# Inner columns of eight experts in chunks of 2048 and 1536 instead of 1024, 1024, 1024 and 512

## The chip, the cores and the metric

The kernel runs on one NeuronCore of a Trainium2 chip. The metric is the time of one execution on the device in microseconds (us). TensorE (PE in the profile) multiplies, PEld is its loading of the stationary operand, VectorE is DVE, ScalarE is ACT, GpSimd is POOL and SyncE is SP, which in this kernel issues nearly all DMAs. Results of TensorE land in PSUM, of which there are eight banks of 2 KB per partition; everything else lives in SBUF, 128 partitions wide.

## The reference, cut to what matters

One sequence of 256 tokens, 1024 wide, goes through two layers, all in float32. Layer 0 is attention with a sliding window and a dense SwiGLU block. Layer 1 is sparse attention and then a mixture of eight SwiGLU experts, of which each token uses two:

```
D_MODEL, SEQ, D_FF, N_EXPERTS, TOP_K = 1024, 256, 3584, 8, 2
...
# per expert e, for the tokens t that chose it, with weight g[t, e]:
y[t] += g[t, e] * (silu(x[t] @ w_gate[e]) * (x[t] @ w_up[e])) @ w_down[e]
x = layer_norm(alpha * x + y)
```

Each expert has three matrices of 1024 x 3584 numbers, 14 MB each (1 MB here is 1,048,576 bytes). All eight together are 336 MB, all of which are read once.

## The kernel before

About the first 510 us are attention, the dense block and the choice of experts. The rest is `run_experts`, which handles the eight experts one after the other (e0 to e7 in the order in which they run), and a short end with the LayerNorm.

**Tokens.** The tokens of an expert are gathered into a transposed tile Th by a product with a 0/1 matrix (`gather`). An expert has room for 96 or for 64 tokens: in order of running 96, 64, 96, 96, 64, 96, 96, 64. The first 64 are multiplied as "halves", two column ranges of the weights side by side on TensorE, and the last 32, where there are any, as "quarters", four ranges side by side. The helper `two` runs both steps over the same weights and swaps their order from call to call. The quarters of e0 stand behind a condition that was not met in the profiled run.

**Chunks.** The 3584 inner columns are cut by WIDE into chunks. For a chunk the gate product runs over all 1024 rows, then what is late (`finish`: the combination of the expert before, and `turn`, which transposes h, the hidden values, of the chunk before), then ACT applies Silu to the gate product, TensorE runs the up product, DVE multiplies the two into h, and then comes the down product of the chunk before (`back`). So the down product is always one chunk late.

**Loads.** The weights come as parts of up to 2048 columns in each of 128 partitions, 1 MB, into a rotation of buffers in three pools, raw, more and later. SP's queue issues them in `load` (L173), in the order in which they are needed: gate, up, and down of the chunk before. `take` hands out parts and lets `load` issue the next, up to `ahead` parts in advance, 15 in this stage. A gate or up part of a chunk of 1024 columns has two rows of 4096 bytes per partition, in the chunk of 512 columns four rows of 2048 bytes; a down part has 8192 bytes in a row:

```
order.append((lambda r=r: src()[r:r + n * P, cols], n, width, False, 1, near))
...
src = src().rearrange("(p k) f -> p k f" if near else "(k p) f -> p k f", p=P)
```

Here `near` is true for down alone. A product takes all the parts of its chunk at once, at most four. The names of lines: L1227 is the halves and L1235 the quarters of gate and up, L1252 and L1258 those of down, L1294 the transposes in `turn`, L1295 ACT's copy of them into hTa, L1278 and L1281 Silu, L1286 DVE's product, L1289 its transpose of the quarters' hidden values, L1168 and L1169 the combination, L352 and L353 the LayerNorm at the end.

**Order.** TensorE's order is the order of the program in this stage; those of the other engines are set by the scheduler.

Of the kernel before, what the change touches and what calls it, by code (L numbers as in the profile page):

```python
# [15 lines left out]
OP = mybir.AluOpType  # L16
# [31 lines left out]
WIDE = (1024, 1024, 1024, 512)  # L48
# [36 lines left out]
def trunk(ctx: ExitStack, tc: tile.TileContext, a, out, dbg=None):  # L85
# [57 lines left out]
    def room():  # L143

        state["ahead"] = RAW + sum(kind[3] for kind in extra) - max(WIDE) * KT // PART

# [937 lines left out]
    class Expert:  # L1084
# [63 lines left out]
        def combine(self, ya, yb):  # L1148

            cap = self.cap  # L1150
            y = moe.tile([CAP, D], F32, name="y", bufs=1)[:cap]
# [25 lines left out]
    def run_experts(jobs):  # L1177
# [38 lines left out]

        def gate_up(pa, pb, x, wide):
            T = x.T
            if pb is not None:
                cleared(pb[:, :wide // 4], x)  # L1220
            parts = [w for (w,) in take(KT * wide // PART, 0)]
            n = PART // wide

            def halves():
                for k in range(KT):
                    for h in range(2):
                        PE.matmul(pa[h * CA:(h + 1) * CA, :wide // 2], T[:, k, :CA],  # L1227
                                  parts[k // n][:, k % n, h * wide // 2:(h + 1) * wide // 2],
                                  start=k == 0, stop=k == KT - 1)

            def quarters():
                for k in range(KT):
                    w = parts[k // n][:, k % n].rearrange("p (b q f) -> p q b f", q=4, f=2 * CB)
                    for q in range(4):
                        PE.matmul(pb[q * CB:(q + 1) * CB, :wide // 4].rearrange("p (b f) -> p b f", f=2 * CB),  # L1235
                                  T[:, k, CA:], w[:, q], start=k == 0, stop=k == KT - 1)

            two(x, halves, quarters if pb is not None else None)

        def down(c, hT, ya, yb, x, between=None):  # L1240
# [3 lines left out]
            parts = [w for (w,) in take(n // 2, 0)]  # L1244
# [4 lines left out]
            def halves():  # L1249
                for f in range(n):  # L1250
                    for o in range(2):
                        PE.matmul(ya[o * CA:(o + 1) * CA, :], hT[0][:, f % (n // 2), f // (n // 2), :],  # L1252
                                  parts[f // 2][:, f % 2, o * 512:(o + 1) * 512], **ends(f))

            def quarters():
                for f in range(n):
                    for q in range(4):
# [172 lines left out]
    def job(e):  # L1430
        def follow(c):
            if c == 1 and e + 1 < len(experts):
                experts[e + 1].pick()
# [67 lines left out]
```

## Time and profile before

| what | value |
|---|---|
| median of 3 runs | 1374.52 us (1373.12 to 1375.53) |
| the profiled execution | 1376.65 us, span of its trace 1374.8 us |
| granted TensorE clock, mean | 0.984 of full speed |
| TensorE busy | 1319.6 us, 96% |
| DVE, ACT busy | 441.5 us, 342.8 us |
| bytes moved by DMA | 434.86 MB (of a million bytes) in 129791 packets |

All times come from the profiled execution unless the median is named. Its trace starts with the first instruction, so a place in the program is given as us from the start. The expert stage lies between 514.8 and 1355.7 us, and about 19 us follow it. A busy TensorE is one that has a matmul under way, whichever clock it was granted.

### The profile page before, as it was taken

The page shows a single profiled execution, that of the slowest core. Times are in us where ns is not written, and L with a number is a line of the kernel's source. Part 1 is how long each engine was busy: PE and PEld are TensorE (multiplying, and loading weights), DVE is VectorE, ACT ScalarE, POOL GpSimd, SP SyncE. Part 2 cuts the span into 40 slices and gives each one's busy share as a digit, 9 for nine tenths or more (in the row PEclk, how much of TensorE's full clock was granted, in tenths as well). Part 3 has the DMA queues.
Part 4 walks back from the last instruction along what each step waited for, and adds up shares of the span by engine and source line. Part 5 has one row for each costly group of instructions (what it writes and reads, how often), then busy time and mean ns, then how long its engine had stood idle before and what let it go on. Part 6 is the DMA issues. An engine that isn't in the chain of part 4 may idle for free. (4 is left out here: it accounts for less than half of the span.)

```text
span 1374.8 us, 21889 instructions
## 1 busy us (share of the span) xinstructions
PE 1319.6 (96%) x9035; PEld 756.0 (55%) x9036; DVE 441.5 (32%) x1015; ACT 342.8 (25%) x783; POOL 8.2 (1%) x16
## 2 busy tenths in 40 slices
PE   9999999999999999988889999999999999999994
PEld 6777888888787883432324354454343454435331
DVE  6776555555979853011002001100100100200203
ACT  5755444443558821100001001000101000100100
POOL 0000000000000000000000000000000000000000
PEclk9999999999999999999999999999999999999997
DMA  9515565555364169999999999999999999999994
GB/s 357 186 63 207 175 189 186 186 181 185 124 238 150 63 260 360 408 409 412 407 412 411 405 412 412 408 401 392 414 404 411 413 405 410 411 407 383 412 407 177
DMA packets 129791, 434.86 MB, mean 316 GB/s; under 512 B 11376, under 2 KB 18192, under 8 KB 115728
## 3 DMA queue, kind: packets, MB, share of 16 engines
q1 hardware_dynamic: 123952, 427.81, 80.3%
q10 hardware_dynamic: 5728, 5.50, 1.2%
q8 instruction: 79, 1.29, 0.4%
q14 instruction: 32, 0.26, 0.1%
HBM read 432.23 MB, written 1.05 MB: 315 GB/s over the span
## 5 line engine op out<-in xcount | busy, mean ns | idle before, releaser
L123 DVE TENSOR_TENSOR lo<-raw,hi 128x512 fp32r<-128x512 f32 (+2 forms) x244 | 166.3, 730 | 110.6 <-ACT hi L122 110.6
L1227 PE MATMUL ps<-more,Th 128*64 128x512 f32 (+1 forms) x920 | 188.3, 557 | 4.1 <-DMA more<-in_moe_w_up 2.3
L122 ACT ACTIVATE hi<-raw 128x512 fp32r<-128x512 f32 (+2 forms) x244 | 145.7, 659 | 147.8 <-PE ps L211 133.1
L209 PE MATMUL ps<-hi,Th 128*128 128x512 f32 (+1 forms) x432 | 171.1, 396 | 1.4 <-ACT Th L122 1.4
L211 PE MATMUL ps<-hi,Tl 128*128 128x512 f32 (+1 forms) x432 | 167.3, 388 | 1.4 <-DVE Tl L123 1.4
L210 PE MATMUL ps<-lo,Th 128*128 128x512 f32 (+1 forms) x432 | 167.7, 388 | 0.0
L1286 DVE TENSOR_TENSOR h<-h,ps 128x512 f32<-128x512 f32 (+1 forms) x32 | 19.8, 620 | 357.7 <-PE ps L1227 357.7
L1227 PE MATMUL ps<-later,Th 128*64 128x512 f32 (+1 forms) x680 | 129.4, 526 | 3.3 <-DMA later<-in_moe_w_up 2.1
L1227 PEld LDWEIGHTS ps<-more,Th 128*64 128x64 f32 x920 | 65.3, 138 | 114.9 <-issue 96.3
L1278 ACT ACTIVATE h<-ps 128x512 f32<-128x512 f32 (+1 forms) x32 | 17.4, 543 | 383.8 <-PE ps L1227 367.0
L1252 PE MATMUL ps<-more,hTa 128*64 128x512 f32 x408 | 92.0, 594 | 3.2 <-DMA more<-in_moe_w_down 2.9
L1227 PE MATMUL ps<-raw,Th 128*64 128x512 f32 (+1 forms) x448 | 91.5, 551 | 3.0 <-DMA raw<-in_moe_w_gate 2.5
L209 PEld LDWEIGHTS ps<-hi,Th 128*128 128x128 f32 x432 | 81.6, 189 | 20.5 <-ACT Th L122 2.6
L211 PEld LDWEIGHTS ps<-hi,Tl 128*128 128x128 f32 x432 | 81.5, 189 | 19.9 <-DVE Tl L123 2.5
L210 PEld LDWEIGHTS ps<-lo,Th 128*128 128x128 f32 x432 | 81.6, 189 | 16.3 <-issue 0.2
L1227 PEld LDWEIGHTS ps<-later,Th 128*64 128x64 f32 x680 | 47.5, 137 | 75.4 <-issue 60.3
L1285 DVE TENSOR_TENSOR hb<-hb,ps 128x256 f32<-128x256 f32 (+1 forms) x20 | 7.8, 388 | 212.3 <-PE ps L1235 168.5
L1252 PE MATMUL ps<-later,hTa 128*64 128x512 f32 x312 | 71.0, 596 | 4.3 <-DMA later<-in_moe_w_down 4.0
L1252 PEld LDWEIGHTS ps<-more,hTa 128*64 128x64 f32 x408 | 29.0, 137 | 61.6 <-issue 56.4
L1227 PEld LDWEIGHTS ps<-raw,Th 128*64 128x64 f32 x448 | 31.4, 137 | 55.6 <-issue 44.3
L1235 PE MATMUL ps<-more,Th 128*32 128x256 f32 (+1 forms) x928 | 50.3, 364 | 4.2 <-DMA more<-in_moe_w_gate 4.2
L1252 PEld LDWEIGHTS ps<-later,hTa 128*64 128x64 f32 x312 | 22.1, 137 | 49.2 <-issue 40.8
(260 smaller groups left out, 1370.0 us busy)
## 6 DMA issues: line engine op xcount, KB each, us to landing
more<-in_moe_w_up SPq DMA_DIRECT2D x53, 1024.0 KB, 18.1
more<-in_moe_w_down SPq DMA_DIRECT2D x51, 1024.0 KB, 17.2
more<-in_moe_w_gate SPq DMA_DIRECT2D x50, 1024.0 KB, 19.0
later<-in_moe_w_down SPq DMA_DIRECT2D x38, 1024.0 KB, 16.9
later<-in_moe_w_gate SPq DMA_DIRECT2D x36, 1024.0 KB, 18.2
later<-in_moe_w_up SPq DMA_DIRECT2D x35, 1024.0 KB, 18.4
raw<-in_moe_w_gate SPq DMA_DIRECT2D x26, 1024.0 KB, 20.0
raw<-in_moe_w_up SPq DMA_DIRECT2D x24, 1024.0 KB, 18.6
```

What stands on the lines that cost most here:

```text
L122: state["act"] = ACT.activation(hi, src, AF.Copy)
L123: DVE.tensor_tensor(lo, src, hi.bitcast(F32), op=OP.subtract)
L209: PE.matmul(ps, xh, wh, start=first, stop=False)
L210: PE.matmul(ps, xh, wl, start=False, stop=False)
L211: PE.matmul(ps, xl, wh, start=False, stop=last)
L1227: PE.matmul(pa[h * CA:(h + 1) * CA, :wide // 2], T[:, k, :CA], parts[k // n][:, k % n, h * wide // 2:(h + 1) * wide // 2], start=k == 0, s ...
L1235: PE.matmul(pb[q * CB:(q + 1) * CB, :wide // 4].rearrange("p (b f) -> p b f", f=2 * CB), T[:, k, CA:], w[:, q], start=k == 0, stop=k == KT ...
L1252: PE.matmul(ya[o * CA:(o + 1) * CA, :], hT[0][:, f % (n // 2), f // (n // 2), :], parts[f // 2][:, f % 2, o * 512:(o + 1) * 512], **ends(f))
L1278: ACT.activation(plain(ha, P), paired(ga[:, :wide // 2], P), AF.Silu)
L1285: DVE.tensor_tensor(plain(hb, CB), plain(hb, CB), paired(ub[:, :wide // 4], CB), op=OP.mult)
L1286: DVE.tensor_tensor(plain(ha, P), plain(ha, P), paired(ua[:, :wide // 2], P), op=OP.mult)
```

## The change

WIDE becomes (2048, 1536). A gate or up part is now one row of 8192 or 6144 bytes per partition, so that a part holds 128 rows of a chunk, 1 MB or 768 KB. An expert has 8 + 8 + 6 + 6 gate and up parts and 14 of down, 46 in all, where it had 42. A new constant ATONCE = 4 is the number of parts that a product takes at once: a gate or up product is made in two calls of `two` over four parts each, and a down product in two calls over four (three) parts each. `ahead` stays at 15.

Gate and up of a chunk now need two PSUM banks for the halves and one for the quarters each, where they had one and one; h, hTa and hTb are twice as wide and have one buffer instead of two. `turn` makes 8 or 6 transposes in two banks. The next expert's gather, which stood between the third chunk's down and the last chunk, now stands right before that expert's first gate product. The load of the LayerNorm's gain and bias stays at the end of the last chunk of the last expert. The tiles that sort the tokens share a buffer with y, to make room.

```diff
-WIDE = (1024, 1024, 1024, 512)
+WIDE = (2048, 1536)
+ATONCE = 4
...
-        state["ahead"] = RAW + sum(kind[3] for kind in extra) - max(WIDE) * KT // PART
+        state["ahead"] = RAW + sum(kind[3] for kind in extra) - ATONCE
...
+        def spans(n):
+            return slice(0, 512), slice(512, n)
         def gate_up(pa, pb, x, wide):
             T = x.T
             if pb is not None:
                 cleared(pb[:, :wide // 4], x)
-            parts = [w for (w,) in take(KT * wide // PART, 0)]
-            n = PART // wide
-            def halves():
-                for k in range(KT):
-                    for h in range(2):
-                        PE.matmul(pa[h * CA:(h + 1) * CA, :wide // 2], T[:, k, :CA],
-                                  parts[k // n][:, k % n, h * wide // 2:(h + 1) * wide // 2],
-                                  start=k == 0, stop=k == KT - 1)
-            def quarters():
-                for k in range(KT):
-                    w = parts[k // n][:, k % n].rearrange("p (b q f) -> p q b f", q=4, f=2 * CB)
-                    for q in range(4):
-                        PE.matmul(pb[q * CB:(q + 1) * CB, :wide // 4].rearrange("p (b f) -> p b f", f=2 * CB),
-                                  T[:, k, CA:], w[:, q], start=k == 0, stop=k == KT - 1)
-            two(x, halves, quarters if pb is not None else None)
+            for k0 in range(0, KT, ATONCE):
+                parts = [w[:, 0, :] for (w,) in take(ATONCE, 0)]
+                def halves():
+                    for k, w in enumerate(parts, k0):
+                        for ps, s in zip(pa, spans(wide // 2)):
+                            for h in range(2):
+                                PE.matmul(ps[h * CA:(h + 1) * CA, :s.stop - s.start], T[:, k, :CA],
+                                          w[:, h * wide // 2 + s.start:h * wide // 2 + s.stop],
+                                          start=k == 0, stop=k == KT - 1)
+                def quarters():
+                    for k, w in enumerate(parts, k0):
+                        w = w.rearrange("p (b q f) -> p q b f", q=4, f=2 * CB)
+                        for q in range(4):
+                            PE.matmul(pb[q * CB:(q + 1) * CB, :wide // 4].rearrange("p (b f) -> p b f", f=2 * CB),
+                                      T[:, k, CA:], w[:, q], start=k == 0, stop=k == KT - 1)
+                two(x, halves, quarters if pb is not None else None)
         def down(c, hT, ya, yb, x, between=None):
             if yb is not None and c == 0:
                 cleared(yb[:, :256], x)
             n = WIDE[c] // P
-            parts = [w for (w,) in take(n // 2, 0)]
             def ends(f):
                 return dict(start=c == 0 and f == 0, stop=c == len(WIDE) - 1 and f == n - 1)
-            def halves():
-                for f in range(n):
-                    for o in range(2):
-                        PE.matmul(ya[o * CA:(o + 1) * CA, :], hT[0][:, f % (n // 2), f // (n // 2), :],
-                                  parts[f // 2][:, f % 2, o * 512:(o + 1) * 512], **ends(f))
-            def quarters():
-                for f in range(n):
-                    for q in range(4):
-                        PE.matmul(yb[q * CB:(q + 1) * CB, :256], hT[1][:, f, :],
-                                  parts[f // 2][:, f % 2, q * 256:(q + 1) * 256], **ends(f))
-            two(x, halves, quarters if yb is not None else None, between)
+            for f0 in (0, n // 2):
+                parts = [w for (w,) in take(n // 4, 0)]
+                def halves():
+                    for i in range(n // 2):
+                        f = f0 + i
+                        for o in range(2):
+                            PE.matmul(ya[o * CA:(o + 1) * CA, :], hT[0][:, f % (n // 2), f // (n // 2), :],
+                                      parts[i // 2][:, i % 2, o * 512:(o + 1) * 512], **ends(f))
+                def quarters():
+                    for i in range(n // 2):
+                        f = f0 + i
+                        for q in range(4):
+                            PE.matmul(yb[q * CB:(q + 1) * CB, :256], hT[1][:, f, :],
+                                      parts[i // 2][:, i % 2, q * 256:(q + 1) * 256], **ends(f))
+                two(x, halves, quarters if yb is not None else None, between if f0 else None)
...
-                ga, gb = bank(), bank() if rest else None
+                ga, gb = [bank() for _ in range(2)], bank() if rest else None
                 gate_up(ga, gb, x, wide)
                 finish()
-                ha = later.tile([P, 512], F32, name="h", bufs=2)[:, :wide // 2]
-                hT = [later.tile([P, 4, 2, CA], F32, name="hTa", bufs=2)[:, :wide // 256]]
-                ACT.activation(plain(ha, P), paired(ga[:, :wide // 2], P), AF.Silu)
+                ha = later.tile([P, 1024], F32, name="h", bufs=1)[:, :wide // 2]
+                hT = [later.tile([P, 8, 2, CA], F32, name="hTa", bufs=1)[:, :wide // 256]]
+                for ps, s in zip(ga, spans(wide // 2)):
+                    ACT.activation(plain(ha[:, s], P), paired(ps[:, :s.stop - s.start], P), AF.Silu)
                 if rest:
-                    hb = later.tile([P, 256], F32, name="hb", bufs=1)[:, :wide // 4]
+                    hb = later.tile([P, 512], F32, name="hb", bufs=1)[:, :wide // 4]
                     ACT.activation(plain(hb, CB), paired(gb[:, :wide // 4], CB), AF.Silu)
-                ua, ub = bank(), bank() if rest else None
+                ua, ub = [bank() for _ in range(2)], bank() if rest else None
                 gate_up(ua, ub, x, wide)
                 if rest:
                     DVE.tensor_tensor(plain(hb, CB), plain(hb, CB), paired(ub[:, :wide // 4], CB), op=OP.mult)
-                DVE.tensor_tensor(plain(ha, P), plain(ha, P), paired(ua[:, :wide // 2], P), op=OP.mult)
+                for ps, s in zip(ua, spans(wide // 2)):
+                    DVE.tensor_tensor(plain(ha[:, s], P), plain(ha[:, s], P), paired(ps[:, :s.stop - s.start], P),
+                                      op=OP.mult)
                 if rest:
-                    hT.append(later.tile([P, 8, CB], F32, name="hTb", bufs=2)[:, :wide // P])
+                    hT.append(later.tile([P, 16, CB], F32, name="hTb", bufs=1)[:, :wide // P])
                     DVE.transpose(hT[1].rearrange("p b s -> p (b s)"), hb)
                 def turn(ha=ha, hT=hT, n=wide // 256):
-                    ps = bank().rearrange("p (j q) -> p j q", j=4)
-                    for j in range(n):
-                        PE.transpose(ps[:, j, :], ha[:, j * P:(j + 1) * P], ident)
-                    ACT.activation(hT[0], ps[:, :n].rearrange("p j (h s) -> p j h s", h=2), AF.Copy)
+                    for j0 in range(0, n, 4):
+                        m = min(4, n - j0)
+                        ps = bank().rearrange("p (j q) -> p j q", j=4)[:, :m]
+                        for j in range(m):
+                            PE.transpose(ps[:, j, :], ha[:, (j0 + j) * P:(j0 + j + 1) * P], ident)
+                        ACT.activation(hT[0][:, j0:j0 + m], ps.rearrange("p j (h s) -> p j h s", h=2), AF.Copy)
...
+    sorting = moe.tile([P, D], F32, name="sorting", tag="y", bufs=1)
+    is_at, tmp = (sorting[:, k * NE * NE:(k + 1) * NE * NE].rearrange("p (a b) -> p a b", a=NE) for k in range(2))
+    key, rank = (sorting[:, k * 128:k * 128 + NE] for k in (1, 2))
...
+            if c == 0 and e + 1 < len(experts):
+                experts[e + 1].pick()
             if c == 1 and e + 1 < len(experts):
-                experts[e + 1].pick()
-            if c == 2 and e + 1 < len(experts):
                 experts[e + 1].gather()
-            if c == 3 and e + 1 == len(experts):
+            if c == 1 and e + 1 == len(experts):
                 del extra[:]
                 load_more()
-            if e == 0 and c == 2:
+            if e == 0 and c == 0:
```

With the new chunks, the loads on SP's queue stand in another order. These are SP's rows before the change, from e0's first parts to e1's first gate part (rows without a number are in order; rows that load or compare registers are left out as "..."):

```order
L173 DMA raw<-in_moe_w_gate 128x2x1024 x4
L173 DMA raw<-in_moe_w_up 128x2x1024 x3
L173 DMA more<-in_moe_w_up 128x2x1024
...
L173 DMA later<-in_moe_w_gate 128x4x512 x2
...
L173 DMA raw<-in_moe_w_up 128x4x512 x2
...
L173 DMA raw<-in_moe_w_down 128x2048
L173 DMA more<-in_moe_w_down 128x2048
...
L173 DMA more<-in_moe_w_down 128x2048 x2
...
L173 DMA more<-in_moe_w_gate 128x2x1024
```

And after, the same place:

```order
L174 DMA raw<-in_moe_w_gate 128x2048 x7
...
L174 DMA more<-in_moe_w_up 128x2048 x5
...
L174 DMA later<-in_moe_w_gate 128x1536 x3
...
L174 DMA later<-in_moe_w_up 128x1536 x3
...
L174 DMA later<-in_moe_w_down 128x2048 x2
...
L174 DMA raw<-in_moe_w_down 128x2048 x3
L174 DMA more<-in_moe_w_down 128x2048
...
L174 DMA more<-in_moe_w_down 128x2048 x2
L174 ISA
L174 DMA more<-in_moe_w_gate 128x2048
```

Before, the last chunk's parts and four of down stand ahead of the next expert's gate, and two of down remain; now eight of down stand there, and six remain.

TensorE's rows at the start of e5, the sixth expert to run, a 96-token one behind a 64-token one. Before (the last two rows of e4's down and e5's gate and up product; the second number of a shape is the columns of one matmul):

```order
L1252 MATMUL ps<-more,hTa 64x512 x16
L1235 MATMUL ps<-more,Th 32x256 x8
L1235 MATMUL ps<-later,Th 32x256 x24
L1227 MATMUL ps<-more,Th 64x512 x4
L1227 MATMUL ps<-later,Th 64x512 x12
L1294 MATMUL ps<-cf,h 128x128 x2
L1227 MATMUL ps<-later,Th 64x512 x8
L1227 MATMUL ps<-raw,Th 64x512 x8
L1235 MATMUL ps<-later,Th 32x256 x16
L1235 MATMUL ps<-raw,Th 32x256 x16
```

After, from the end of the gather that now stands in front:

```order
L1145 MATMUL ps<-shares,pickb 96x3
L1241 MATMUL ps<-later,Th 32x512 x16
L1233 MATMUL ps<-later,Th 64x512 x20
L1233 MATMUL ps<-raw,Th 64x512 x12
L1241 MATMUL ps<-later,Th 32x512 x4
L1241 MATMUL ps<-raw,Th 32x512 x12
L1309 MATMUL ps<-cf,h 128x128 x6
L1241 MATMUL ps<-more,Th 32x512 x16
L1233 MATMUL ps<-more,Th 64x512 x28
```

The quarters (L1241) and the halves (L1233) of a gate product now alternate over its two groups of four parts, and six transposes of e4's last chunk (L1309) stand where two did.

ACT's rows in a 96-token expert, where a chunk follows another. Before:

```order
L1281 ACTIVATE hb<-ps 128x256
L1278 ACTIVATE h<-ps 128x512
L1295 ACTIVATE hTa<-ps 128x512
L1278 ACTIVATE h<-ps 128x512
L1281 ACTIVATE hb<-ps 128x256
```

After, from the end of a gather on, with the Silu of the quarters into hb and of the halves into h:

```order
L1142 ACTIVATE back<-ps 96x256
L1292 ACTIVATE hb<-ps 128x512
L1310 ACTIVATE hTa<-ps 128x512
L1310 ACTIVATE hTa<-ps 128x256
L1289 ACTIVATE h<-ps 128x512 x2
```

The copies into hTa now come before the Silu of the halves, and there are two of each.

## Rows read from the trace of the kernel before

**Rows 1.** The page's first part: the span, and TensorE's busy time.

```profile
span 1374.8 us, 21889 instructions
...
PE 1319.6 (96%) x9035; PEld 756.0 (55%) x9036; DVE 441.5 (32%) x1015; ACT 342.8 (25%) x783; POOL 8.2 (1%) x16
```

**Rows 2.** Stretches: busy us of each engine, granted clock, DMA share, GB/s.

```profile
527.00:698.00 171.00, 152.22 (x778) 59.60 (x774) 16.70 (x44) 13.16 (x28) 0.00 (x0) 1.00 1.02 409
527.00:1353.00 826.00, 796.57 (x6252) 341.31 (x6248) 77.32 (x167) 65.99 (x132) 0.00 (x0) 0.99 1.02 407
702.00:711.00 9.00, 6.87 (x46) 2.25 (x44) 0.00 (x0) 0.38 (x1) 0.00 (x0) 0.62 1.03 410
716.00:1024.00 308.00, 308.00 (x2654) 138.06 (x2654) 31.12 (x66) 26.46 (x52) 0.00 (x0) 1.00 1.02 407
1043.00:1336.00 293.00, 293.00 (x2550) 129.14 (x2548) 29.09 (x56) 24.08 (x47) 0.00 (x0) 1.00 1.02 406
```

**Rows 3.** TensorE's waits, 690 to 1375 us: total us, times, longest.

```profile
PE ps L1235 <- DMA more<-in_moe_w_gate: 4.2, 4, 1.5
PE ps L1235 <- DMA later<-in_moe_w_gate: 3.9, 3, 1.5
...
PE ps L1252 <- DMA later<-in_moe_w_down: 1.8, 3, 0.7
```

**Rows 4.** Stretches with one packet size, as in rows 2.

```profile
634.00:641.00 7.00, 5.44 (x26) 1.54 (x24) 0.69 (x1) 0.00 (x0) 0.00 (x0) 1.00 1.01 421
721.00:738.00 17.00, 17.00 (x174) 6.93 (x172) 2.96 (x5) 2.79 (x5) 0.00 (x0) 1.00 1.02 408
672.00:681.00 9.00, 7.88 (x54) 5.03 (x56) 0.23 (x2) 0.72 (x2) 0.00 (x0) 1.00 1.03 386
```

**Rows 5.** TensorE's timeline in e1: start, us, instruction, wait before it.

```profile
644.63 1.94 PE L1252 MATMUL ps<-later,hTa 128*64 128x512 f32 x8 [0.59 <-DMA later<-in_moe_w_down]
...
665.05 1.94 PE L1227 MATMUL ps<-more,Th 128*64 128x512 f32 x8 [0.59 <-DMA more<-in_moe_w_up]
...
675.05 1.94 PE L1252 MATMUL ps<-more,hTa 128*64 128x512 f32 x8 [0.58 <-DMA more<-in_moe_w_down]
```

**Rows 6.** TensorE's timeline from e2's start on.

```profile
698.51 1.07 PE L1235 MATMUL ps<-more,Th 128*32 128x256 f32 x16 [0.70 <-DMA more<-in_moe_w_gate]
...
707.98 8.13 PE L1227 MATMUL ps<-more,Th 128*64 128x512 f32 x32
...
754.33 3.64 PE L1258 MATMUL ps<-more,hTb 128*32 128x256 f32 x64
757.89 7.09 PE L1252 MATMUL ps<-more,hTa 128*64 128x512 f32 x32
```

**Rows 7.** TensorE's timeline at e5's start.

```profile
1024.68 1.07 PE L1235 MATMUL ps<-more,Th 128*32 128x256 f32 x16
1026.68 1.07 PE L1235 MATMUL ps<-later,Th 128*32 128x256 f32 x16 [0.93 <-DMA later<-in_moe_w_gate]
...
1042.72 0.44 PE L1294 MATMUL ps<-cf,h 128*128 128x128 f32 x2
```

**Rows 8.** TensorE's timeline at the first gate products of e3 and e4.

```profile
822.86 1.46 PE L1227 MATMUL ps<-raw,Th 128*64 128x512 f32 x6
...
941.75 1.46 PE L1227 MATMUL ps<-later,Th 128*64 128x512 f32 x6
```

**Rows 9.** The timeline of all engines at the end of the stage.

```profile
1318.34 0.66 PE L1294 MATMUL ps<-cf,h 128*128 128x128 f32 x4
...
1319.03 0.60 ACT L1295 ACTIVATE hTa<-ps 128x512 f32<-128x512 f32 x1
...
1327.77 0.35 ACTq L324 DMA_DIRECT2D more<-in_ln_gain  x1
...
1354.66 1.08 PE L1252 MATMUL ps<-raw,hTa 128*64 128x512 f32 x4 [0.18 <-SPq L1449]
...
1366.09 1.41 DVE L352 SCALAR_TENSOR_TENSOR acc<-acc,mv,more 128x512 f32<-128x512 f32 x2
```


## What the change will do to the time: the prediction

> **What bounds the kernel now.** I read the page first: TensorE is busy in 1319.6 of 1374.8 us [rows 1], an average that hides two regimes, so the table of stretches comes next. From 527 us to 1353 us the DMA engines never rest (share 1.02, 407 GB/s) [rows 2], so this part, the experts, cannot end before their bytes are in. The same table splits it: up to 698 us TensorE is busy in 152.22 of 171.00 us, waiting for each part; from 716 to 1024 and from 1043 to 1336 us, 601 us together, it has no gap at all [rows 2]. So in the first two experts (e0, e1) the stream sets the pace, and from the third (e2) on TensorE does, except where a gate product finds its parts missing. The list of TensorE's waits names two such places, 4.2 us at e2's start and 3.9 us at e5's, and 1.8 us for down's last parts [rows 3]. A faster stream can be cashed only up to 698 us, in those two holes, and in the last waits.
>
> **What a transfer costs.** Three rates stand in stretches that one kind fills nearly alone: 421 GB/s for down's 8192-byte packets, 408 for gate and up in 4096, 386 in the last chunk's 2048 [rows 4]. Where TensorE waits for each part, the starts of its groups give the same: four down parts from 665.05 to 675.05, 2.50 us each; eight of up and gate from 644.63 to 665.05, 2.553 each [rows 5]. Between both readings I take 2.495 us per MB (1,048,576 bytes) at 8192, 2.56 at 4096, and 2.716 at 2048. 6144 bytes do not occur. 128 packets fewer per MB saved 0.065 us from 4096 to 8192; 6144 means 43 more than 8192, so 2.517, an estimate between the ends 2.495 and 2.56.
>
> The Trainium skill (DMA: Bandwidth & Descriptors, section "Why small descriptors are slow (HBM only)") has a fixed overhead of about 3 cycles per packet beside beats of 32 bytes. By it the step from 4096 to 8192 would be worth 1.2%; the rows show 2.6 to 3%, so I go by the rows. An estimate by that rule for the whole change is 7 us off the stream, not 16.
>
> **The change, part by part.**
> 1. *Packets.* Gate and up carry 224 MB over eight experts. Before: 192 x 2.56 + 32 x 2.716 = 578.4 us. After: 128 at 8192 and 96 at 6144 bytes, 128 x 2.495 + 96 x 2.517 = 561.0. Sixteen parts are loaded before the stream is saturated (16 x 0.065 = 1.0), so the stream ends 16.4 us earlier. That SP issues 46 transfers per expert instead of 42 I cost at nothing, since one lands only every 1.9 to 2.5 us.
> 2. *e2's start.* Down of a chunk is loaded one chunk late. Before e2's first gate part the old order brings 66 MB after the first sixteen, the new one 62, since 6 MB of e1's down wait instead of 2. Before: 32 x 2.56 + 8 x 2.716 + 26 x 2.495 = 168.5 us (the stretch took 171). After: 38 x 2.495 + 24 x 2.517 = 155.2. So e2 begins 13.3 us earlier, near 685. But 4 MB more of down are still to be multiplied, 7.1 us [rows 6], and the catch-up there is about 1 us longer, since the hole repeats: the first step over four parts waits for the fourth, and the granted clock falls behind such gaps (0.62 of 2.4 GHz over 702 to 711 us, so mostly the lower level of 1.2) [rows 2], by which a product of 7.1 us took 8.13 [rows 6]. Net -5.2 us.
> 3. *e5's start.* 1024.68 to 1042.72 is 18.0 us [rows 7] for a product of 3.64 + 7.09 = 10.7 [rows 6]: 7.3 us of waits and half clock. After: the stream stands 13.3 us earlier at e2 and gains per expert 24 x 2.56 + 4 x 2.716 against 16 x 2.495 + 12 x 2.517, 2.2 us, so 19.9 at e5. TensorE comes there 12.3 us earlier (e4 leaves the same 4 MB of down behind that e1 left, 7.1 us more and 7.1 less). The part for which TensorE waited from 1025.75 on came at 1026.68; it now comes at 1006.8, the fourth by 1012, and TensorE at 1012.4. The hole closes, -7.3 us, just about.
> 4. *The end.* The 1.8 us of waits [rows 3], and as an estimate as much again for up's last part and the fill of groups that stand apart, fall away if the stream is ahead: -3.5.
> 5. *Sum.* -5.2 - 7.3 - 3.5 = -16.0 for TensorE and -16.4 for the stream: both limits together. Against both stand the buffers. "Ahead" is 15 parts before and after, but a 1536 part is three quarters of one. A 96-token expert keeps TensorE 941.75 - 822.86 = 118.9 us [rows 8] while its 28 MB take 105, so the stream's lead grows by 14 us per such expert, 28 over e2 and e3, and by some 8 in e2's hole: 36 us. Fifteen parts are worth 15 x 2.495 = 37 us, all of 1536 columns 28, in their mixture about 33. Where the lead reaches that, the stream pauses, for 0 to 8 us, and it needs that lead later, in the 64-token experts, where TensorE is the faster one. In the old order 15 parts always held 38 us and the lead reached 2 x (118.9 - 107.2) + 7 = 30. TensorE pays only what of a pause reaches e5 and the end: I take 1.5 us, near the lower end, since 8 of the 36 us come from a hole that is itself uncertain, and a pause costs only what then lacks at e5; both ends, 0 and 8, go into the range.
> 6. *Costed at nothing.* The same columns pass TensorE, in 512- and 256-wide pieces as now. h and hTa have one buffer instead of two, and ACT copies two banks of transposes before Silu: its 0.60 us each [rows 9] lie under the up product, whose first banks were not read by Silu; the cover is 3.6 us and more of TensorE's quarters or other halves, and without it the price is that of the slower rival. hTb has one buffer too: DVE's transpose now waits for the previous down, and behind it stand only adds that come after the next gate. The gather stands one chunk earlier and keeps its length. "sorting" shares y's buffer, done before the first combine. Gain and bias, 1 MB on ACT's queue, now stand behind the last copies of transposes and ahead of the last y, so that they are issued about 10 us before TensorE ends instead of 27 [rows 9]; they are wanted 10.4 us behind its end (1355.74 to 1366.09) [rows 9], so 20 us cover them. If not, two MB-times at most, 5 us.
>
> So -14.5 us. The profiled execution took 1376.65 us and would take 1362.1; it lay 2.1 above the median 1374.52, and so I say 1360.0.
>
> **The rivals.**
> A. *Buffers bind* (chance 0.13). A pause of 5 to 9 us is paid in full, at e5 and at the end: 1363.5 to 1367.5. For: 36 us of lead against 33 of buffer. Against: no wait of TensorE on a transfer between 716 and 1024 us now, when the lead was 30.
> B. *8192 bytes help only where a part is one contiguous MB* (0.07). Down's are; gate's are rows cut out of wider ones. Then only the 2048-byte packets go: 32 x (2.716 - 2.56) = 5.0 us off the stream. e2 starts 11.2 us earlier (4 MB and 8 x 0.156), for 7.1 and 1 more work; e5's hole mostly stays. 1370.5.
> E. *A packet costs half of what I take* (0.04): 0.25 ns instead of 0.51, with 2.495 at 8192 kept, so 2.528 at 4096, 2.593 at 2048 and 2.506 at 6144. The stream gains 568.4 - 560.0 - 0.5 = 7.9 us and is the limit: 1366.6. Against: 386 GB/s at 2048 [rows 4], where it would be 404. The rule of the Trainium skill named above is of this size.
> C. *All is cashed* (0.08). No pause, and the holes shrink more than I count: -16.5 to -19, 1355.5 to 1358.
> D. *Slower: TensorE stalls between gate and up* (0.09). A chunk's gate and up fill two banks and one each, with down's two that is all eight; if up's first bank is one that Silu has still to read, TensorE waits behind the transposes for two copies and two Silus, 4 x 0.60 us less the second half of the transposes (0.66 per four [rows 9]), about 2 to 2.5 us in each of the 12 chunks from e2 on: +24 to +30, less 14.5, near 1387. From 1.2 us per chunk on it decides. Against: by the order of allocation up's banks are those that the gather's share, "back" and the quarters had, which ACT empties first.
>
> **Chances and range.** The likeliest, 1357 to 1363, has 0.59. With A, C, E and a little of B it makes faster 0.85. 0.2% is 2.7 us, about what a measurement here can tell, so the same is 1371.8 to 1377.3: the rest of B and a D of some 1.2 us per chunk, 0.08. Slower 0.07, the rest of D. The range 1355.5 to 1369 holds A, C and E and leaves out B and D, 0.16.
>
> **What would show it.** In the changed profile: rates of 415 to 421 GB/s in gate and up (B: 408); e2's first product near 685; no waits of a gate product at e5; the last part landing near 1337; PE ending near 1341; no wait of L1233 or L1241 on ACT (D). The prediction is wrong if the stream's rate is not above 410, or if TensorE shows gaps of over 1 us between gate and up.

## The result, and the profile after

The changed kernel took 1360.51 us (median of 4 runs, 1358.55 to 1361.03) beside 1374.26 us of the kernel before on the same chip, a ratio of 0.9901 with a 95% interval of 0.9889 to 0.9912. The forecast was 1360.0.

The page of the profile after has these lines; the last but one are the 40 slices of 34 us with the DMA rate of each:

```profile
span 1359.2 us, 19868 instructions
...
PE 1307.9 (96%) x8007; PEld 726.1 (53%) x8012; DVE 437.0 (32%) x991; ACT 337.4 (25%) x773; POOL 8.2 (1%) x16
...
GB/s 354 191 68 194 180 187 185 185 186 186 134 203 202 32 278 281 414 419 417 418 420 417 417 419 418 413 420 418 417 419 419 416 419 419 397 409 419 416 419 169
DMA packets 97526, 434.71 MB, mean 320 GB/s; under 512 B 11888, under 2 KB 18704, under 8 KB 67088
```

From the seventeenth slice on the stream runs at 413 to 420 GB/s, where it had 407 [rows 2], except for 397 and 409 near 1155 to 1220 us. The table of stretches (columns as in [rows 2]) has first a stretch with three quarters of its bytes in 8192-byte packets and one quarter in 6144, one with 6144-byte parts nearly alone, and then the start of the expert stage:

```profile
715.00:745.00 30.00, 30.00 (x170) 9.46 (x164) 2.77 (x4) 1.09 (x3) 0.00 (x0) 1.00 1.01 418
1280.00:1300.00 20.00, 20.00 (x147) 9.29 (x144) 4.90 (x9) 2.63 (x4) 0.00 (x0) 1.00 1.02 416
...
527.00:540.00 13.00, 12.70 (x60) 4.78 (x58) 0.00 (x0) 1.68 (x3) 0.00 (x0) 1.00 0.86 337
510.00:560.00 50.00, 48.02 (x238) 21.84 (x240) 13.96 (x65) 7.70 (x14) 0.00 (x0) 0.93 0.83 324
```

418 and 416 GB/s are 2.51 and 2.52 us per MB, against 408 [rows 4] before. The same two stretches at the start had more in the kernel before, which the rows ahead of the prediction don't show:

```profile
527.00:540.00 13.00, 12.47 (x60) 4.65 (x58) 1.92 (x5) 1.36 (x3) 0.00 (x0) 1.00 1.01 415
510.00:560.00 50.00, 47.97 (x222) 19.92 (x222) 13.63 (x66) 5.96 (x12) 0.00 (x0) 0.94 0.87 345
```

So the new stream starts later into its full rate: 21 GB/s over 50 us are 1.05 million bytes, 2.5 us of stream (2.9 us if the 45 us from each kernel's first gate product on are compared, 346 against 373 GB/s).

TensorE's timeline after, at the first gate product of e0, at e2's start, at the gathers of e3's and e4's start, at e5's start and at the end:

```profile
514.21 8.54 PE L1233 MATMUL ps<-raw,Th 128*64 128x512 f32 x32
...
685.05 1.94 PE L1261 MATMUL ps<-more,hTa 128*64 128x512 f32 x8 [0.56 <-DMA more<-in_moe_w_down]
686.92 3.81 PE L1129 MATMUL ps<-pick,x 128*128 128x96 f32 x32
...
690.82 2.78 PE L1241 MATMUL ps<-more,Th 128*32 128x512 f32 x24
695.03 1.07 PE L1241 MATMUL ps<-later,Th 128*32 128x512 f32 x8 [1.43 <-DMA later<-in_moe_w_gate]
...
713.48 0.87 PE L1309 MATMUL ps<-cf,h 128*128 128x128 f32 x6
...
801.57 0.69 PE L1129 MATMUL ps<-pick,x 128*128 128x96 f32 x4
...
919.64 0.55 PE L1129 MATMUL ps<-pick,x 128*128 128x64 f32 x3
...
1009.50 2.78 PE L1241 MATMUL ps<-later,Th 128*32 128x512 f32 x24
1013.34 1.06 PE L1241 MATMUL ps<-later,Th 128*32 128x512 f32 x8 [1.06 <-DMA later<-in_moe_w_gate]
...
1031.80 0.88 PE L1309 MATMUL ps<-cf,h 128*128 128x128 f32 x6
...
1332.99 1.08 PE L1261 MATMUL ps<-raw,hTa 128*64 128x512 f32 x4 [0.71 <-DMA raw<-in_moe_w_down]
1335.37 1.08 PE L1261 MATMUL ps<-raw,hTa 128*64 128x512 f32 x4 [1.31 <-DMA raw<-in_moe_w_down]
1336.90 1.08 PE L1261 MATMUL ps<-raw,hTa 128*64 128x512 f32 x4 [0.45 <-DMA raw<-in_moe_w_down]
...
1339.33 1.08 PE L1261 MATMUL ps<-more,hTa 128*64 128x512 f32 x4 [0.18 <-SPq L1464]
```

The list of TensorE's waits from 690 us on answers to [rows 3]:

```profile
PE ps L1241 <- DMA later<-in_moe_w_gate: 2.5, 2, 1.4
PE ps L1261 <- DMA raw<-in_moe_w_down: 2.5, 3, 1.3
PE ps L1169 <- ACT Tl L1160: 1.9, 1, 1.9
PE ps L1241 <- DMA more<-in_moe_w_gate: 0.5, 1, 0.5
```

The 8.1 us of gate waits have become 3.0, those for down are still there. SP's queue, between 1155 and 1220 us, where the stream is slowest (401 GB/s), waits for TensorE:

```profile
SPq L174 <- PE ps L1233: 18.1, 9, 7.2
SPq L174 <- PE ps L1241: 15.6, 6, 5.4
```

The last group of matmuls starts at 1339.33 instead of 1354.66 [rows 9], 15.3 us earlier. Of these 0.6 us lie ahead of the stage: e0's first gate product started at 514.21 instead of 514.82. Three of the four groups ahead of the last one waited for their bytes (0.71, 1.31, 0.45 us), so the stream still ends last, if by little. How TensorE came there: its first gate product of e2 starts at 690.82 instead of 698.51 [rows 6], -7.7, with the gather now in front of it. That product takes 713.48 - 690.82 = 22.7 us for twice 10.7, a hole of 1.2 us. Before, from 698.51 to the end of the halves at 707.98 + 8.13 = 716.1 [rows 6], it was 17.6 for 10.7, a hole of 6.9, so -5.7. Four MB more of down: +7.1. From e2's to e5's first gate product another 1.8 us are saved, since e5's stands at 1009.50 instead of 1024.68 [rows 7], -15.2 in all: e3, a 96-token expert, takes 919.64 - 801.57 = 118.1 us from gather to gather where 118.9 lay between its first gate product and the next [rows 8]. The hole at e5 is 1031.80 - 1009.50 - 21.4 = 0.9 us instead of 7.3, -6.4. The rest to the end is -0.8: together -15.3.

### The profile page after: what moved, and what is told of

Read it like the earlier page. It is cut to its first block, busy times and chain, and to the rows that moved or that the text cites. A ratio compares the mean times of both kernels' runs of the same rounds, so it can differ in the third digit from the quotient of the medians.

```text
span 1359.2 us, 19868 instructions
## 1 busy us (share of the span) xinstructions
PE 1307.9 (96%) x8007; PEld 726.1 (53%) x8012; DVE 437.0 (32%) x991; ACT 337.4 (25%) x773; POOL 8.2 (1%) x16
## 3 DMA queue, kind: packets, MB, share of 16 engines
HBM read 432.23 MB, written 1.05 MB: 319 GB/s over the span
## 5 line engine op out<-in xcount | busy, mean ns | idle before, releaser
L1233 PE MATMUL ps<-more,Th 128*64 128x512 f32 (+1 forms) x944 | 185.5, 542 | 3.8 <-DMA more<-in_moe_w_up 2.2
L1233 PE MATMUL ps<-later,Th 128*64 128x512 f32 (+1 forms) x664 | 130.0, 539 | 1.7 <-DMA later<-in_moe_w_up 1.1
L1233 PEld LDWEIGHTS ps<-more,Th 128*64 128x64 f32 x944 | 67.4, 137 | 116.4 <-issue 98.8
L1233 PE MATMUL ps<-raw,Th 128*64 128x512 f32 (+1 forms) x440 | 89.8, 550 | 3.2 <-DMA raw<-in_moe_w_up 1.5
L1233 PEld LDWEIGHTS ps<-later,Th 128*64 128x64 f32 x664 | 48.5, 137 | 80.0 <-issue 68.6
L1261 PE MATMUL ps<-later,hTa 128*64 128x512 f32 x296 | 66.6, 595 | 4.3 <-DMA later<-in_moe_w_down 3.2
L1130 ACT ACTIVATE Th<-ps 128x384 f32<-128x384 f32 (+1 forms) x14 | 6.2, 445 | 243.1 <-PE ps L1129 243.1
L1154 ACT ACTIVATE y<-ps 64x512 f32<-64x512 f32 x16 | 9.5, 592 | 222.5 <-PE ps L1261 222.3
L1233 PEld LDWEIGHTS ps<-raw,Th 128*64 128x64 f32 x440 | 31.8, 139 | 57.7 <-issue 47.7
L1241 PE MATMUL ps<-more,Th 128*32 128x512 f32 (+1 forms) x472 | 48.8, 543 | 0.5 <-DMA more<-in_moe_w_gate 0.5
L1261 PE MATMUL ps<-raw,hTa 128*64 128x512 f32 x192 | 44.4, 597 | 4.2 <-DMA raw<-in_moe_w_down 4.0
## 6 DMA issues: line engine op xcount, KB each, us to landing
more<-in_moe_w_gate SPq DMA_DIRECT2D x40, 768.0 KB, 16.4
```

Source lines behind the costliest of these rows:

```text
L1130: ACT.activation(self.T[:, 4 * h:4 * h + 4, :], ps, AF.Copy)
L1154: ACT.activation(y[:CA, o * 512:(o + 1) * 512], ya[o * CA:(o + 1) * CA, :], AF.Copy)
L1233: PE.matmul(ps[h * CA:(h + 1) * CA, :s.stop - s.start], T[:, k, :CA], w[:, h * wide // 2 + s.start:h * wide // 2 + s.stop], start=k == 0, ...
```

## The experiments

**Theory 1:** the gain is the stream's. Wider packets bring the bytes earlier, TensorE's holes only decide where it waits, and what the buffers hold back is lost. **Theory 2:** the gain is the order's, that is, less of the stream ahead of e2 and a gather that fills the hole. A rival of its own concerns the gather, and the last experiments the buffers. All edits are against the changed kernel unless the kernel before is named.

**1. The changed kernel with narrow packets.** Each chunk consists of two column ranges:

```diff
-                f = slice(f0, f0 + wide)
-                f0 += wide
-                plan_later(wg, slice(0, D), f)
-                plan_later(wu, slice(0, D), f)
+                f = slice(f0, f0 + wide // 2)
+                f0 += wide // 2
+                for w1 in (wg, wu):
+                    for r in range(0, D, P):
+                        order.append((lambda w1=w1, r=r: w1()[r:r + P, :], 2, wide // 2, False, 1, f))
...
+                back = [(wd, slice(f.start + g, f.stop + g), slice(0, D), True) for g in (0, 1792)]
```

> The changed kernel with its chunks, order of loads, buffers and products, but each chunk made of two column ranges 1792 apart, so that a gate or up part of 1 MB comes in packets of 4096 bytes and one of 768 KB in packets of 3072. Theory 1, the wider packets carry the gain: gate and up take 128 x 2.56 + 96 x 2.604 (3072 bytes by the same 0.51 ns per packet) = 577.7 us instead of 561.0, which is what they took before the change, so the stream ends 16 us later and the time goes back to 1373 to 1377. Theory 2, the new order carries it (4 MB less ahead of e2, the gather where the parts are missing): 1361 to 1365, near the changed kernel.

Measured: 1377.89 us, ratio to the kernel before 1.0026 (1.0016 to 1.0036), so nothing of the gain is left, and theory 2's 1361 to 1365 is out; the time lies 0.9 us above theory 1's range. Its table of stretches, for 4096- and for 3072-byte parts:

```profile
706.00:726.00 20.00, 20.00 (x128) 6.40 (x126) 0.00 (x0) 2.45 (x5) 0.00 (x0) 1.00 1.02 411
1067.00:1083.00 16.00, 14.08 (x86) 4.77 (x84) 1.41 (x2) 2.41 (x4) 0.00 (x0) 0.89 1.03 398
```

411 GB/s, with an eighth of the bytes still in 8192-byte packets, is near the 408 [rows 4] that 4096-byte packets had before, and 398 (2.63 us per MB; 2.604 was expected) shows the next step down. That the same order of work with these packets is even slower than the old cut fits its late start and smaller parts, but was not tried apart.

**2. The stream alone, before (2a) and after (2b).** In both, seven experts are cut to 64 tokens, and the pass for left-over tokens is gone:

```diff
-CAPS = tuple(CA if 0 < r < 4 else CAP for r in RANKS)
+CAPS = tuple(CA if e else CAP for e in range(8))
```

> The kernel before, with seven of the experts cut to 64 tokens, so that the quarters of e2, e3, e5 and e6 and the pass for left-over tokens are left out: TensorE has less to do than the stream takes in every expert, and the time shows the stream alone. By the rates of the trace the stream from the seventeenth part on takes 578.4 + 279.4 - 16 x 2.56 = 816.8 us and ends near 1346 to 1349, the time near 1367 to 1370. If TensorE set the pace of the kernel before by its own work, the time falls further, below 1362.

> The changed kernel with the same work left out. Theory 1: 561.0 + 279.4 - 16 x 2.495 = 800.5 us of stream, so 16 us less than the kernel before with the same cut, near 1351 to 1354. Theory 2, in which the stream gains little and the order does: less than 8 us between the two.

Measured: 1367.28 us and 1355.94 us, 11.3 apart: more than theory 2's 8, less than theory 1's 16; 2a lies in its range, 2b 1.9 us above its own. One long stretch of each, 2a's first, shows the rates as forecast:

```profile
570.00:1330.00 760.00, 625.33 (x3044) 220.37 (x3040) 51.22 (x105) 54.18 (x107) 0.00 (x0) 1.00 1.02 410
...
570.00:1330.00 760.00, 638.58 (x3074) 221.80 (x3070) 49.81 (x98) 50.99 (x107) 0.00 (x0) 1.00 1.01 418
```

8 GB/s of 418 over 800 us are 15.3 us; the start takes some back, in 2b as in the changed kernel (336 GB/s over 527 to 540 us, 414 in 2a). What is worth reading here: four experts of 2a have 30% less for TensorE to do (82.9 us, from 941.75 to 1024.68, instead of 118.9 [rows 7, 8]), and it is only 7 us faster than the kernel before, whose stream alone gives 1367.28.

**3. The gather one chunk earlier.**

```diff
+            if c == 0 and e == 0:
+                experts[1].pick()
             if c == 0 and e + 1 < len(experts):
-                experts[e + 1].pick()
-            if c == 1 and e + 1 < len(experts):
                 experts[e + 1].gather()
+            if c == 1 and e + 2 < len(experts):
+                experts[e + 2].pick()
```

> The changed kernel with the gather of the next expert one chunk earlier (behind the first chunk's products instead of right before the next gate product) and the choice of its tokens earlier still. Theory 1: at e2 the first step of the gate product waits for the fourth part, which lands at 695 us whether the gather stands in between or not, and elsewhere the 3.9 us of the gather only change place: within 1 us of the changed kernel. Rival: the gather now stands on the path of each expert's start and covers nothing: 3 to 5 us faster, from e2 and e5.

Measured: 1363.66 us, ratio 0.9923 (0.9905 to 0.9940), not faster, so the rival is out. The median is 3.2 us above the changed kernel's, where theory 1 had 1; the intervals overlap a little (0.9889 to 0.9912 for the changed kernel). It fits that its stream has 385 instead of 410 GB/s over 540 to 560 us, where the gather now stands in e0, and 382 instead of 413 in the 26th slice, 3.7 us of stream together; this was not tried apart. Its timeline at e2:

```profile
685.69 1.07 PE L1241 MATMUL ps<-more,Th 128*32 128x512 f32 x8 [0.65 <-DMA more<-in_moe_w_gate]
...
693.08 1.93 PE L1241 MATMUL ps<-later,Th 128*32 128x512 f32 x8 [1.44 <-DMA later<-in_moe_w_gate]
...
712.98 0.88 PE L1309 MATMUL ps<-cf,h 128*128 128x128 f32 x6
```

The product starts 5.1 us earlier and ends at 712.98 instead of 713.48: each part is waited for (0.65, 1.33, 1.42 and 1.44 us), which is the hole that the prediction saw. The gather in the changed kernel costs nothing there because it stands in that hole.

**4. The kernel before with the gather late.**

```diff
-            if c == 2 and e + 1 < len(experts):
+            if c == 3 and e + 1 < len(experts):
                 experts[e + 1].gather()
```

> The kernel before, with one thing of the change: the gather of the next expert stands right before that expert's first gate product instead of one chunk earlier. In the changed kernel the gather ran while the first gate parts of e2 came in, and the holes at e2 and e5 shrank. Theory 1, the stream ends when it ends: a hole that is filled at e2 or e5 only makes TensorE wait longer for the last parts, at most 2 us faster, 1372 to 1375. Theory 2, filling the holes is a good part of the gain: 4 to 7 us faster, 1367 to 1370.

Measured: 1373.16 us, ratio 0.9990 (0.9978 to 1.0001). The transposes behind the gate product, at 716.04 and 1042.72 [rows 7] in the kernel before, come 3.4 and 4.4 us earlier:

```profile
712.67 0.44 PE L1294 MATMUL ps<-cf,h 128*128 128x128 f32 x2
...
1038.36 0.44 PE L1294 MATMUL ps<-cf,h 128*128 128x128 f32 x2
```

TensorE is ahead by that and gives most of it back, waiting for the last bytes. From 690 us on its waits for gate parts are 2.8 us in all instead of 8.1 [rows 3], but those for up and down 8.5 instead of 3.8. The two longest of them:

```profile
PE ps L1252 <- DMA more<-in_moe_w_down: 2.3, 4, 0.6
PE ps L1227 <- DMA more<-in_moe_w_up: 2.1, 2, 1.2
```

Filling the holes is not the gain.

**5. Chunks of 2048, 1024 and 512.**

```diff
-WIDE = (2048, 1536)
+WIDE = (2048, 1024, 512)
...
+            n = max(1, PART // wide)
+            for k0 in range(0, KT, ATONCE * n):
+                parts = [w[:, j, :] for (w,) in take(min(ATONCE, KT // n), 0) for j in range(n)]
```

The gather keeps its place right before the next expert's first gate product, and `spans` cuts a range into pieces of at most 512 columns.

> The changed kernel with chunks of 2048, 1024 and 512, so packets of 8192, 4096 and 2048 bytes, all parts of 1 MB. By packets alone gate and up take 128 x 2.495 + 64 x 2.56 + 32 x 2.716 = 570.1 us, half way between 578.4 and 561.0, and the start of the stage is not short of bytes: theory 1 gives 8 to 9 us less than the kernel before, 1365 to 1367. Theory 2, the two chunks as such carry the gain: 1370 and more, since three chunks with one of 512 are nearly the old cut.

Measured: 1367.66 us, ratio 0.9940 (0.9919 to 0.9962), 0.7 us above the range given: about half of the gain for half of the packets' gain. At the start, where whole parts of 1 MB follow the first sixteen, the stream runs at 410 GB/s over 527 to 540 us, not at 337.

**6. Chunks of 1536 and then 2048.** The edit is `WIDE = (1536, 2048)`.

> The changed kernel with its chunks the other way round, 1536 and then 2048: the same bytes in the same packets, but the parts that wait in the buffers when the stage starts are of 768 KB, 12 MB instead of 16. Theory 1, the stream's end sets the time and its start belongs to it: 4 MB at 2.495 us each have to come later, so up to 10 us longer, 1366 to 1371. Theory 2, TensorE sets the time from e2 on and the stream has slack: the stream brings 2 MB less ahead of e2, and the time is 1357 to 1362.

Measured: 1374.85 us, ratio 1.0001 (0.9990 to 1.0011). Theory 2 is out again, but theory 1 had the loss in the wrong place, and too small. The profiled execution took 1380.33 us, the longest of ten, so the sizes that follow are those of a long one. The start is better, not worse (363 GB/s over 510 to 560 us, and 421 over 527 to 540 us, where parts of 1 MB follow). The loss stands where TensorE works through 96-token experts:

```profile
895.00:953.00 58.00, 58.00 (x456) 26.71 (x454) 4.55 (x10) 2.88 (x7) 0.00 (x0) 1.00 0.91 361
1236.00:1321.00 85.00, 85.00 (x580) 37.15 (x578) 7.54 (x14) 7.36 (x15) 0.00 (x0) 1.00 0.95 379
```

Against 419 GB/s these are 8.0 and 8.1 us of stream. SP's own list of waits between 895 and 953 us (total us, times, longest) says for what:

```profile
SPq L174 <- PE ps L1233: 14.0, 11, 4.8
SPq L174 <- PE ps L1241: 7.9, 3, 7.3
```

SP waits for TensorE's products to give buffers back, up to 7.3 us at a time, and for that long its queue starts no transfer. So the buffers bind, and by more than the 1.5 us of the forecast's term.

**7. Two parts less ahead.** The edit is `- ATONCE - 2` for `- ATONCE` in `room`.

> The changed kernel with 13 parts ahead instead of 15, in the same buffers. Theory 1, the buffers already bind (337 GB/s at 527 to 540 us where the kernel before has 415, and 397 in one slice around e6): two parts less cost up to 5 us of stream at the start and a longer pause behind e2 and e3, e5 and e6: 1364 to 1369. Theory 2, there are parts to spare: within 1 us of the changed kernel.

Measured: 1368.44 us, ratio 0.9950 (0.9931 to 0.9969), 8 us slower than the changed kernel. Over 527 to 540 us the stream falls to 294 GB/s, and two slices fall to 366 and 372:

```profile
GB/s 355 192 63 206 175 187 185 184 181 184 142 211 180 55 255 302 415 419 416 419 418 418 417 419 414 366 420 418 416 419 420 416 419 419 372 402 419 416 419 181
...
527.00:540.00 13.00, 12.70 (x60) 4.71 (x58) 0.00 (x0) 1.68 (x3) 0.00 (x0) 1.00 0.80 294
```

At the start this costs little, 318 instead of 324 GB/s over 510 to 560 us, 0.7 us of stream. The slices of 366, 372 and 402, where the changed kernel has 413, 397 and 409, cost 6.5 us: they lie in the second of two 96-token experts in a row (e3 and e6).

**8. Parts by twos, and by ones.** A product takes two parts (or one) at a time, so that 17 (or 18) are ahead in the same buffers:

```diff
-ATONCE = 4
+ATONCE = 2
...
-            for f0 in (0, n // 2):
-                parts = [w for (w,) in take(n // 4, 0)]
+            m = 2 * ATONCE
+            for f0 in range(0, n, m):
+                parts = [w for (w,) in take(ATONCE, 0)]
```

> The changed kernel with parts taken by twos instead of by fours in every product, so that two parts fewer are held by TensorE and 17 instead of 15 are ahead in the same buffers; the same packets and products, halves and quarters only swap twice as often. Theory 1, the buffers hold the stream back at the start (337 GB/s at 527 to 540 us) and behind two 96-token experts in a row (397 GB/s in one slice): taking two parts away cost 8 us, so two more give back what is left of it, 3 to 6 us: 1354 to 1358. Theory 2, 15 were enough and TensorE sets the rest: within 1.5 us of the changed kernel, 1359 to 1362.

> As by twos, with single parts and 18 ahead. Theory 1: about 1 us below the kernel by twos if the stream still pauses there, otherwise the same, since the stream's bytes and TensorE's work are both used up. Rival: with a change between halves and quarters at each part TensorE loses time, 2 us or more above the kernel by twos.

Measured: 1354.49 us by twos, ratio 0.9859 (0.9844 to 0.9874), 6.0 us faster than the changed kernel and the fastest of all; 1365.42 us by ones, ratio 0.9943 (0.9929 to 0.9956). By twos the start and the slow slices are mended:

```profile
GB/s 356 195 65 195 180 187 186 186 186 186 132 195 216 32 268 326 418 419 417 419 419 418 417 419 418 417 419 418 417 419 420 416 419 419 413 419 419 414 417 148
...
510.00:560.00 50.00, 47.74 (x230) 20.58 (x232) 13.37 (x63) 7.32 (x14) 0.00 (x0) 0.94 0.92 369
```

369 instead of 324 GB/s over 50 us are 2.25 million bytes, 5.4 us of stream (4.8 if both are counted from the first gate product, 390 against 346 GB/s over 45 us). By ones the start gains a little more (386 GB/s over 510 to 560 us), and TensorE loses: the pages have it busy for 1311.1 us by twos and for

```profile
PE 1326.3 (97%) x8011; PEld 712.2 (52%) x8012; DVE 437.1 (32%) x991; ACT 337.2 (25%) x773; POOL 8.2 (1%) x16
```

by ones, with the same matmuls. From 690 us on its list of TensorE's waits has none for a transfer: here TensorE sets the time. It is the rival that was named.

**9. The kernel before by twos.** The same edit in the old `gate_up` and `down`, with 17 parts ahead.

> The kernel before, with parts taken by twos and 17 ahead. Theory 1, it was not held back by its buffers (15 parts of 1 MB are 38 us of stream, its lead reaches 30) and the stream was saturated from 527 us: at most 3 us faster, from the holes at e2 and e5 that a step over two parts shortens, 1371 to 1375. Theory 2, parts by twos are worth as much here as in the changed kernel, because they shorten the holes: 1367 to 1370.

Measured: 1366.52 us, ratio 0.9949 (0.9936 to 0.9963): 7.8 us faster, and theory 1's reading of the kernel before falls. Theory 2 had nearly the size (0.5 us below its range), but not the place, since experiment 4 fills the holes and gains 1.2 us, hardly more than the noise. Its stretch at the start:

```profile
510.00:560.00 50.00, 47.58 (x212) 17.06 (x214) 11.45 (x61) 5.84 (x12) 0.00 (x0) 0.97 0.99 393
```

393 instead of 345 GB/s are 2.4 million bytes, 5.8 us of stream at the 408 to 415 that it runs at. Part of this is no effect of the edit: the first gate product of this execution stands at 511.07 instead of 514.82 us. Over the 45 us from that product on it is 400 instead of 373 GB/s, 3.0 us. The rest stands at the end of the second of two 96-token experts in a row (e3 and e6, whose successors' gathers start at 915.83 and 1242.51 us), where the kernel before has these stretches:

```profile
920.00:944.00 24.00, 24.00 (x304) 13.24 (x298) 1.44 (x6) 1.55 (x5) 0.00 (x0) 1.00 0.98 371
1237.00:1272.00 35.00, 35.00 (x420) 20.20 (x418) 1.18 (x4) 2.29 (x6) 0.00 (x0) 1.00 0.99 383
```

By twos the same places have 411 (916 to 940 us) and 410 GB/s, so these are 2.3 us each, and 7.6 with the start. The kernel before, too, had been held back, at the start of the stage by a first step that gave no buffer back before four parts were through, and where TensorE has worked through two 96-token experts, while SP waits for it. But the change keeps its worth with either grain: by twos it takes 1366.52 to 1354.49, 12.0 us, by fours 13.75.

## Why the prediction came out right, point by point

**Packets: right.** 8192 and 6144 bytes run at 418 and 416 GB/s, 2.51 and 2.52 us per MB where 2.495 and 2.517 were taken. Experiment 1 takes the packets away and the gain with them, and 5 takes half of either. Rival B is out, since gate and up do not stay at 408 GB/s, and so is E, whose steps are half as large: 398, 408 to 411 and 418 GB/s at 3072, 4096 and 8192 bytes are steps of 2.5 to 3.3% and 1.7 to 2.5%. By the rule of the Trainium skill (DMA: Bandwidth & Descriptors, "Why small descriptors are slow (HBM only)"), an overhead of about 3 cycles per packet beside beats of 32 bytes, the same steps would be an estimated 0.8% and 1.2%; these traces do not agree.

**The stream's end: 16.4 forecast, 15.3 measured,** 0.6 of it ahead of the stage. The step that failed is "sixteen parts are loaded before the stream is saturated", as if it were saturated from 527 us after the change as well. Parts of 768 KB now follow there, each in the buffer of a whole part: 337 GB/s instead of 415, and 2.5 us lost. Where whole parts follow, 410 (5) and 421 (6), the loss is not there.

**e2's start: right in sum, wrong in its parts.** -13.3 + 1 was forecast for start and hole, -7.7 - 5.7 = -13.4 was measured. "The hole repeats" was wrong, and with it "the gather stands one chunk earlier": it keeps its length, as forecast, but stands later, between down and the expert's first gate product, 3.8 us in which parts land. It delays the start and takes away the hole; experiment 3 puts both back, and the end of the product moves by 0.5 us.

**e5's start: right.** -7.3 forecast, -6.4 measured, with 1.06 us of waiting left; TensorE came there 15.2 instead of 12.3 us earlier, 1.8 of it because e2, e3 and e4 take 0.6 us less each on average, which was costed at nothing. It fits that the old chunk of 512 ran its products in narrower pieces (3.67 us for the halves of two parts, where half of a product of four is 3.5); this was not tried apart.

**The end: wrong.** -3.5 was forecast if the stream is ahead. It is not: -0.8 was left, and the waits for the last parts are still 0.71 + 1.31 + 0.45 us.

**The buffers: mis-sized, and luck in the sum.** The term was 1.5 us "between 0 and 8". Two parts less cost 8 us and two more give 6, so they hold back about 6 us of what the packets could give. The sum came out since the kernel before was held back as well, by 7.8 us (9), where the forecast had "15 parts always held 38 us" against a lead of 30 and so no pause at all. (An expert has 42 MB, not the "28 MB" of that term; its 105 us are right for 42.) The comparison sees only the difference of two such losses: by twos the change is worth 12.0 us, by fours 13.75, so the buffers added about 1.8 us to the gain where the forecast took 1.5 off. That this difference is small is luck, not something the forecast derived. Rival A was half right: the buffers bind, but the comparison hardly sees it.

**The slower rival D: not seen.** The list of waits after has none of L1233 or L1241 on ACT; its one long wait for ACT, 1.9 us, is at the combination behind the stage, as before the change.

Left open is why the 1536 chunk first (6) costs 16 us of stream in its profiled execution, when the order of the chunks decides what lies in the buffers behind two 96-token experts: the places are shown, the bookkeeping of parts there is only argued.

## What to carry to other kernels

Where TensorE shows no gap for 600 us, the stream can still be what ends last: a kernel that is given 30% less work in half of its experts and gets only 7 us faster says so more plainly than the list of waits, which has a few us. A change of part sizes is then to be costed in bytes that the buffers hold, at the start of the stage and behind the work that gives buffers back most slowly, before and after the change, and each part that a product takes at once is one that cannot be ahead. Work that moves onto the spot where a product waits for its bytes is free there, and gains nothing if the stream ends last.

## What was not expected of the hardware

A swap between the 64-wide and the 32-wide form of the products is not free: by ones, each of the four 96-token experts swaps after every part, and TensorE is busy for 15.2 us more (1326.3 against 1311.1) with the same 8011 matmuls. An expert has 32 gate and up parts (8 + 8 + 8 + 8) and 14 of down, so 46 steps by ones, 23 by twos and 12 by fours. From e3's gather to e4's, by twos and by ones:

```profile
796.29 3.81 PE L1129 MATMUL ps<-pick,x 128*128 128x96 f32 x32
...
915.95 3.79 PE L1129 MATMUL ps<-pick,x 128*128 128x64 f32 x32
...
797.89 3.81 PE L1129 MATMUL ps<-pick,x 128*128 128x96 f32 x32
...
920.85 3.79 PE L1129 MATMUL ps<-pick,x 128*128 128x64 f32 x32
```

These are 119.7 and 123.0 us, where the changed kernel takes 118.1: about 0.14 us for each further pair of steps, both times. It is the swap and not the smaller step, since from e4's gather to e5's, where 64 tokens need no quarters but for the last down parts of e3, it is 86.0, 86.0 and 86.5 us by fours, twos and ones.
